# Rotary turn in a two-layer hybrid kernel: rows swapped by SBUF transfers in place of a product with a constant matrix

## The chip, the cores and the metric

The kernel runs on one core of a Trainium2 chip, as one launch. The metric is the time on the device in microseconds (us); less is better. The engines are named as in the profile: PE (TensorE, matrix products), PEld (its weight loads), DVE (VectorE), ACT (ScalarE), POOL (GpSimd) and SP (SyncE, which here only issues transfers).

## What is computed

Two layers run over 512 latent tokens and 256 context tokens of width 1024. Each layer is: a half-step SwiGLU, a token mixer, and a second half-step SwiGLU, each with a modulation in front and a layer norm behind. Mixer 0 is a neighbourhood attention. Mixer 1 is a windowed attention of 16 query heads over 4 key heads, and its queries and keys are turned by a rotary embedding that depends on the row and the column of the token:

```python
def rot(xa, pos):
    ang = pos[:, None] * inv_freq[None, :]
    cos = jnp.cos(ang)[None, :, None, :].astype(x.dtype)
    sin = jnp.sin(ang)[None, :, None, :].astype(x.dtype)
    x1, x2 = xa[..., :n], xa[..., n:]
    return jnp.concatenate([x1 * cos - x2 * sin, x2 * cos + x1 * sin], axis=-1)

return jnp.concatenate([rot(x[..., :half], rows), rot(x[..., half:], cols)], axis=-1)
```

A head has 64 dimensions; `half` is 32 and `n` is 16. So within every block of 32 dimensions the upper 16 and the lower 16 change places, those that move up take a minus sign, and the result is multiplied by the sine; the tile itself, multiplied by the cosine, is added. Everything is float32 in the reference.

## The kernel before

Activations lie with the feature dimension on the 128 partitions and the tokens along the free dimension. Large products are done in three passes (`mm3`, lines 162 to 166): both factors are split into a high and a low part of a faster type, and high x high, high x low and low x high are summed in PSUM. Weights come from HBM in quarters of 128 x 512 (256 KB) through SP's queue (`raw_quarter`, line 94), and are split by ACT (line 102) and POOL (line 104) into a ring of eight pairs; five raw buffers (`RAWS`) and this ring (`RING`) set how far SP can load ahead.

Mixer 1 is `wa_mixer`. Its stages:

- V of the latent tokens (`v_tiles`), then two K tiles of 128 x 512 (two heads each), each projected (`wk`, lines 163 to 166), turned by `rope`, split and copied to both halves of the partitions by `stack_k` (lines 845 to 849);
- `proj(0)`: two Q tiles (`wq`), each turned by `rope` and split by `stack_q` (lines 838 to 841); then K and V of the context tokens (`wkc`, `vw`). In this stage the layer norm of the context tokens and its modulation (lines 317 to 322, 480) also run;
- for `u` from 0 to 2: attention of two head pairs with the Q at hand (`attn`: score products at lines 1156 to 1163 and 853/854, softmax on DVE and ACT, scaling at line 893, transposes at line 877, products with V at line 886), then `proj(u + 1)`, two more Q tiles, then the output projection of the heads that were just done (`wo_pairs`, tile `pow`, lines 163 to 166, added to the residual at line 495);
- attention of the last two head pairs and their output projection.

So `rope` is called ten times: for two K tiles and eight Q tiles. It copies the projection from PSUM to SBUF with its scale (`qe`, ACT, line 1098), multiplies the constant matrix `rm_sb` (a signed permutation, 128 x 128, float32) with it on PE (line 1100, the result in the PSUM bank pair `mm`, which the projections use too), multiplies that by the sine table `rc[1]` on DVE (line 1102), multiplies `qe` in place by the cosine table `rc[0]` on POOL (line 1103), and adds the two on DVE (line 1104).

The order of the instructions on every engine and on SP's queue is not the order of the source. The framework plans it before the run with a timing model of its own (`schedule_with_timeline_sim=True`): an instruction is placed when the model has its inputs and its buffer ready, earlier lines of the source first. On the chip every engine, and SP, then goes through its list strictly in order, and waits where an input is late. The helper `behind` adds constraints on the order, and `plan`/`at` put pieces of the layer norms at named points.

Constants are loaded by `constants()`, called by `late_gate` in the first SwiGLU (`ffn("0a", ...)`), while `gemv_dve`, a background stream of DVE products for the modulation (line 211), runs. That stream keeps two PSUM banks, tags `o` and `t`, for the conditioning vector (`cb`, written by ACT at line 235); the tag `t` has a single bank.

Temporary tiles of 128 x 512 come from pools by tag: `t2` has six buffers, `ln` two (`t2()`, lines 53 and 54).

Of the kernel before, what the change touches and what calls it, by code (L numbers as in the profile page):

```python
# [8 lines left out]
F32 = mybir.dt.float32  # L9
# [4 lines left out]
ALU = mybir.AluOpType  # L14
# [4 lines left out]
P = 128  # L19
D = 1024  # L20
# [18 lines left out]
def hybrid_kernel(ctx: ExitStack, tc: tile.TileContext, h0, cc, crow, wmod, wmodt, bmod, lnp, wst,  # L39
                  rpbp, nmask, sinks, ropec, rmat, ident, wmask, out):  # L40
    nc = tc.nc
    cp = ctx.enter_context(tc.tile_pool(name="cp", bufs=1))
# [7 lines left out]
    def bank(tag, nm):  # L50
        return pp.tile([P, 512], F32, tag=tag, name=nm, bufs=banks[tag])

    def t2(nm, tag="t2"):
        return tp.tile([P, 512], F32, tag=tag, name=nm, bufs={"t2": 6, "ln": 2, "sl": 2}[tag])
# [11 lines left out]
    nmask_sb = cp.tile([P, 3, 32], F32, name="nmask_sb")  # L66
    nsink = cp.tile([P, NH], F32, name="nsink")
    rm_sb = cp.tile([P, P], F32, name="rm_sb")
    onesd = cp.tile([P, P], F32, name="onesd")
    nc.vector.memset(onesd[:], 1.0 / D)  # L70
    zero = cp.tile([P, 4], F32, name="zero")
# [266 lines left out]
    def behind(x, y):  # L338

        if y is not None and x.ins.engine == y.ins.engine:  # L340
            tc.add_manual_dep(x.ins, y.ins.name, mybir.DependencyInfo(
                mybir.DependencyClass.NoSync, mybir.DependencyReason.DATA), reason="order")
# [559 lines left out]
    def constants():  # L902
        for t, src in ((lnp_sb, lnp), (nmask_sb, nmask), (rm_sb, rmat)):
            behind(nc.sync.dma_start(t[:], src[:]), loaded[0])
        nc.sync.dma_start(nsink[:], sinks[:].broadcast_to([P, NH]))
        nc.vector.tensor_scalar(out=nsink[:], in0=nsink[:], scalar1=-1.0, scalar2=None, op0=ALU.mult)

    def bias_tables():
        for r in range(8):
            behind(nc.sync.dma_start(xd[:, r], rpbp[:, :, 7 - r:15 - r]), loaded[0])  # L910
# [173 lines left out]
    def wa_mixer(gt):  # L1084
        phase("S")
        rc = []
        for i in range(2):
            t = gp.tile([P, NL], F32, tag="gs", name=f"rc{i}", bufs=6)
# [3 lines left out]
        nc.sync.dma_start(mk[:, 0:256], wmask[:])  # L1092
        nc.vector.tensor_copy(mkb[:].rearrange("p a b -> p (a b)"), mk[:, 0:256])

        def rope(nm, ps, scale):

            qe = t2(f"qe{nm}")
            nc.scalar.activation(qe[:], ps[:], AF.Copy, scale=scale)
            pr = bank("mm", f"pr{nm}")
            nc.tensor.matmul(pr[:], rm_sb[:], qe[:], start=True, stop=True)  # L1100
            sn = t2(f"sn{nm}")
            nc.vector.tensor_tensor(out=sn[:], in0=pr[:], in1=rc[1][:], op=ALU.mult)
            nc.gpsimd.tensor_tensor(out=qe[:], in0=qe[:], in1=rc[0][:], op=ALU.mult)
            nc.vector.tensor_tensor(out=sn[:], in0=qe[:], in1=sn[:], op=ALU.add)
            return sn

        iv = wpos[0]
        vt = v_tiles("w", wunit(), range(4), ("mm", "c"))
# [2 lines left out]
        for i in range(2):  # L1111
            ps = bank("s", f"wk{i}")
            mmk(ps[:], w, i * P, 0, NL)
            at(f"wk{i}")
            stack_k(*ks[i], 0, NL, rope(f"k{i}", ps, 1.0))

        def proj(u):
            w = wunit()
            qs = []
            for i in range(2):  # L1120
                ps = bank("mm", f"wq{u}_{i}")
                mmk(ps[:], w, i * P, 0, NL)
                at(f"wq{u}_{i}")
                sl = [slab(f"wq{u}_{i}_{x}") for x in range(2)]
                stack_q(*sl, 0, NL, rope(f"q{u}_{i}", ps, -0.125), 1.0)
                qs.append(sl)
            return qs

        qs = proj(0)
        for i in range(2):  # L1130
            ps = bank("mm", f"wkc{i}")
# [121 lines left out]
    with tc.tile_pool(name="pre", bufs=1) as fp:  # L1253
        open_av()
        for q in range(4):
            pieces = []
            for i in range(2):
                t = fp.tile([P, 4, 512], F32, tag="wm", name=f"wm0_{q}_{i}", bufs=7)
# [75 lines left out]
    def late_gate():  # L1334
        gemv_dve(0, (16, 20, (0, 1)), (20, 24, (0, 1)), (40, 72, (0, 1)), (24, 40, (0, 1)))
        for _ in range(33):
            next(bg[0][1])
        bg[0] = (bg[0][0] - 33, bg[0][1])
        constants()

    def whole(x, head):
# [23 lines left out]
    plan(wo6_2=l4[0][:1], wo6_3=l4[0][1:2], wm7_3=l4[0][2:3], pow3_1_256_1=l4[0][3:4], pow3_1_256_5=l4[0][4:6],  # L1365
         pow3_1_256_7=l4[1][:1])
    wa_mixer(gate(1, 5, 1.0))
    plan(pa1b_0_0_0=l4[0][6:], pv1b_0_0_0=l4[1][1:3], pd1b_0_0_3=l4[1][3:4], pd1b_0_0_7=l4[1][4:])
    ffn("1b", g1, lambda: gate(1, 8, 0.5), None, final, apart=True)
# [126 lines left out]
```

## Time and profile before

| | |
|---|---|
| time, median of 3 runs | 2771.27 us (2769.65 to 2777.23) |
| span of the profiled execution (from the first to the last instruction; the page gives no other time of it) | 2767.9 us |
| PE busy, share of the span | 2668.7 us, 96% |
| DVE busy | 1869.2 us, 68% |
| POOL busy | 1683.2 us, 61% |
| ACT busy | 1202.4 us, 43% |
| mean granted TensorE clock | 0.987 |
| first and last start of a rotary product | 2089.9 us and 2294.9 us |

All times in the profile are microseconds from the start of the span, unless marked ns. In rows of instructions, the first number is the start and the second the duration, then engine, line, operation, `output<-inputs`, shapes, and `xcount` where several were merged; square brackets give the idle time of the engine just before and what ended it. A name followed by `q` (SPq, ACTq) is the engine's queue: the issue of a transfer, not the transfer. Matmuls are pipelined, so their durations overlap; the distance from one start to the next is the cost of one. The clock is granted by a throttle; 1.00 is full speed.

### The profile page before, as it was taken

To read this page: it belongs to the slowest core of one execution; us is meant where nothing else is said; L and a number is where in the kernel's file an instruction comes from. 1 tells how busy PE (TensorE), PEld (TensorE's weight loads), DVE (VectorE), ACT (ScalarE), POOL (GpSimd) and SP (SyncE) were. 2 spreads that over 40 slices of the span, in tenths; PEclk is the share of its full clock that TensorE was granted. 3 is DMA by queue.
4 is the path that set the end of the run, shared out by engine and by line. 5 is a ranking of instruction groups with operands and counts; after the bars stand their busy time and mean duration, and the time that the engine had idled before them with its cause. 6 is when DMAs were issued, how large, how long until landed. Compare 5 with 4: busy or idle time off the path is not lost. (4 is left out here: it accounts for less than half of the span.)

```text
span 2767.9 us, 47921 instructions
## 1 busy us (share of the span) xinstructions
PE 2668.7 (96%) x16954; PEld 2419.6 (87%) x16954; DVE 1869.2 (68%) x4252; ACT 1202.4 (43%) x2487; POOL 1683.2 (61%) x1530
## 2 busy tenths in 40 slices
PE   8999999999999989999999999999998999899997
PEld 5899998888888888999998899999986777889997
DVE  4877777775555677656556676666587667787765
ACT  4344343366446353443433434343336555444442
POOL 4786766454434556967665577767545445677762
PEclk9999999999999999999999999999999999999998
DMA  9467565421222113454543226465722111235551
GB/s 317 108 172 206 143 157 155 143 81 58 58 58 64 55 49 89 121 136 117 133 133 103 72 85 164 123 163 158 208 83 61 31 32 47 70 96 126 134 143 56
DMA packets 295615, 311.92 MB, mean 113 GB/s; under 512 B 27856, under 2 KB 193872, under 8 KB 294352
## 3 DMA queue, kind: packets, MB, share of 16 engines
q1 hardware_dynamic: 278960, 279.36, 33.5%
q0 software_dynamic: 16128, 29.37, 6.4%
q8 instruction: 134, 2.20, 0.3%
q14 instruction: 105, 0.86, 0.1%
q10 hardware_dynamic: 288, 0.14, 0.0%
HBM read 300.92 MB, written 12.25 MB: 113 GB/s over the span
## 5 line engine op out<-in xcount | busy, mean ns | idle before, releaser
L104 POOL TENSOR_TENSOR wl<-wr,wh 128x512 fp32r<-128x512 f32 x200 | 262.9, 1332 | 148.8 <-ACT wh L102 93.3
L104 POOL TENSOR_TENSOR wl_s<-S,wh_s 128x512 fp32r<-128x512 f32 x240 | 317.7, 1359 | 49.5 <-ACT wh_s L102 48.2
L102 ACT CAST wh_s<-S 128x512 fp32r<-128x512 f32 x256 | 155.3, 620 | 418.2 <-POOL S L620 137.4
L620 POOL TENSOR_TENSOR S<-wr,wr 128x512 f32<-128x512 f32 x128 | 174.2, 1361 | 184.5 <-DMA wr<-in_wst_dram 165.6
L211 DVE CUSTOM_DVE_ANT_0 jk<-wt,cb 128x512 f32<-128x512 f32 x360 | 244.5, 679 | 23.5 <-DMA wt<-in_wmodt_dram 18.6
L104 POOL TENSOR_TENSOR wl_a<-wr,wh_a 128x512 fp32r<-128x512 f32 x144 | 189.7, 1365 | 18.0 <-ACT wh_a L102 14.3
L102 ACT CAST wh_a<-wr 128x512 fp32r<-128x512 f32 x192 | 118.8, 621 | 147.1 <-PE pd1b L165 18.6
L102 ACT CAST wh<-wr 128x512 fp32r<-128x512 f32 x200 | 120.6, 617 | 82.7 <-DMA wr<-in_wst_dram 20.0
L495 DVE SCALAR_TENSOR_TENSOR z<-pd0b,gt,z 128x256 f32<-128x256 f32 (+1 forms) x168 | 97.2, 594 | 42.3 <-PE pd0b L166 41.7
L495 DVE SCALAR_TENSOR_TENSOR z<-pd1a,gt,z 128x512 f32<-128x512 f32 (+1 forms) x160 | 95.6, 614 | 38.5 <-PE pd1a L166 38.2
L893 POOL TENSOR_SCALAR p<-p,l 128x512 f32<-128x512 f32 x64 | 44.3, 694 | 120.3 <-DVE l L1001 114.6
L495 DVE SCALAR_TENSOR_TENSOR z<-pd0a,gt,z 128x512 f32<-128x512 f32 (+1 forms) x160 | 93.5, 611 | 16.2 <-PE pd0a L166 16.1
L335 POOL TENSOR_SCALAR z<-z,ag_None,ab_None 128x256 f32<-128x256 f32 (+1 forms) x78 | 62.3, 802 | 62.1 <-DVE uh L321 47.9
L620 POOL TENSOR_TENSOR S<-S,wr 128x512 f32<-128x512 f32 x64 | 90.5, 1414 | 3.2 <-POOL x1b L562 0.4
L620 POOL TENSOR_TENSOR S<-wr,S 128x512 f32<-128x512 f32 x64 | 90.1, 1408 | 3.5
L893 POOL TENSOR_SCALAR pw<-pw,l 128x512 f32<-128x512 f32 (+1 forms) x64 | 41.0, 641 | 67.2 <-DVE l L1195 24.1
L317 ACT ACTIVATE ufl<-z,bi_None,sc_None 128x256 f32<-128x256 f32 (+1 forms) x86 | 55.1, 655 | 53.6 <-DVE z L480 52.4
L1000 ACT ACTIVATE p<-s,m 128x512 f32<-128x512 f32 x64 | 44.0, 688 | 78.1 <-DVE m L998 72.2
L322 DVE TENSOR_TENSOR ul<-ufl,uh 128x256 fp32r<-128x256 f32 (+1 forms) x88 | 59.9, 687 | 2.6 <-ACT ufl L317 1.3
L211 DVE CUSTOM_DVE_ANT_0 jk<-zspare,cb 128x512 f32<-128x512 f32 x88 | 59.7, 678 | 0.6
L495 DVE SCALAR_TENSOR_TENSOR z<-pd1b,gt,z 128x512 f32<-128x512 f32 (+1 forms) x91 | 53.2, 618 | 9.1 <-PE pd1b L166 8.9
L104 DVE TENSOR_TENSOR wl_a<-wr,wh_a 128x512 fp32r<-128x512 f32 x48 | 53.8, 1134 | 6.7 <-ACT wh_a L102 6.7
(1469 smaller groups left out, 10671.7 us busy)
## 6 DMA issues: line engine op xcount, KB each, us to landing
wr<-in_wst_dram SPq DMA_DIRECT2D x456, 256.0 KB
wt<-in_wmodt_dram SPq DMA_DIRECT2D x206, 256.0 KB
zspare<-in_wmodt_dram SPq DMA_DIRECT2D x50, 256.0 KB
wr_0b<-in_wst_dram SPq DMA_DIRECT2D x47, 256.0 KB
wr_1b<-in_wst_dram SPq DMA_DIRECT2D x47, 256.0 KB
wr_2b<-in_wst_dram SPq DMA_DIRECT2D x47, 256.0 KB
wr_3b<-in_wst_dram SPq DMA_DIRECT2D x47, 256.0 KB
wm<-in_wmod_dram SPq DMA_DIRECT2D x8, 1024.0 KB
```

Of the source, the lines that this page charges most:

```text
L102: nc.scalar.copy(hi[:], src[:])
L104: x = eng.tensor_tensor(out=lo[:], in0=src[:], in1=hi[:].bitcast(F32), op=ALU.subtract)
L211: x = nc.vector.tensor_tensor_reduce(out=junk[:], in0=w[:], in1=cb[st], scale=1.0, scalar=0.0, op0=ALU.mult, op1=ALU.add, accum_out=out[st])
L317: nc.scalar.activation(uf[:, :n], zs, AF.Identity, scale=s1, bias=s2)
L322: return hi, nc.vector.tensor_tensor(out=lo, in0=uv, in1=uo.bitcast(F32), op=ALU.subtract)
L335: nc.gpsimd.tensor_scalar(out=zs, in0=zs, scalar1=prm[2][:, d:d + 1], scalar2=prm[3][:, d:d + 1], op0=ALU.mult, op1=ALU.add)
L495: last[0] = nc.vector.scalar_tensor_tensor(out=zt(d, c0, c1), in0=pd, scalar=gt[:, d, st:st + 1], in1=zt(d, c0, c1), op0=ALU.mult, op1=ALU ...
L620: nc.gpsimd.tensor_tensor(out=t[:], in0=a[:], in1=b[:], op=o)
L893: nc.gpsimd.tensor_scalar(out=p, in0=p, scalar1=r, scalar2=0.0, op0=ALU.mult, op1=ALU.add)
L1000: last_exp[0] = nc.scalar.activation(p[:], ps[:], AF.Exp, bias=m[:, 0:1], scale=-1.0, accum_out=l[:, 0:1])
```

## The change

The matrix product is gone from `rope`. In its place SP issues eight transfers for each tile, from SBUF to SBUF: block `x` of 16 partitions of the new tile `qr` is filled from block `x ^ 1` of `qe`, which is 16 partitions of 2 KB, 32 KB, a transfer. The sine product on DVE then reads `qr` from SBUF instead of the PSUM bank, and writes it in place; POOL writes the cosine product to a tile of its own, `qc`, from the pool `ln`.

The sign, which the matrix held, goes into the sine table: `rc[1]` is multiplied once by a column `sgn` of +1 and -1 on POOL. That column is made in `constants()` by a product of `rm_sb` with a column of `onesd` (whose elements are 1/D) in a bank with the tag `t`, multiplied by D on DVE. The inputs of the kernel and its host code stay as they are.

```diff
@@ constants of the kernel
     rm_sb = cp.tile([P, P], F32, name="rm_sb")
+    sgn = cp.tile([P, 1], F32, name="sgn")
     onesd = cp.tile([P, P], F32, name="onesd")
@@ constants()
         nc.vector.tensor_scalar(out=nsink[:], in0=nsink[:], scalar1=-1.0, scalar2=None, op0=ALU.mult)
+        ps = bank("t", "sgn")
+        nc.tensor.matmul(ps[:, 0:1], rm_sb[:], onesd[:, 0:1], start=True, stop=True)
+        nc.vector.tensor_scalar(out=sgn[:], in0=ps[:, 0:1], scalar1=float(D), scalar2=None, op0=ALU.mult)
@@ wa_mixer()
+        nc.gpsimd.tensor_scalar(out=rc[1][:], in0=rc[1][:], scalar1=sgn[:], scalar2=0.0, op0=ALU.mult, op1=ALU.add)
+
         def rope(nm, ps, scale):
 
-            qe = t2(f"qe{nm}")
+            qe, qr, qc = t2(f"qe{nm}"), t2(f"qr{nm}"), t2(f"qc{nm}", "ln")
             nc.scalar.activation(qe[:], ps[:], AF.Copy, scale=scale)
-            pr = bank("mm", f"pr{nm}")
-            nc.tensor.matmul(pr[:], rm_sb[:], qe[:], start=True, stop=True)
-            sn = t2(f"sn{nm}")
-            nc.vector.tensor_tensor(out=sn[:], in0=pr[:], in1=rc[1][:], op=ALU.mult)
-            nc.gpsimd.tensor_tensor(out=qe[:], in0=qe[:], in1=rc[0][:], op=ALU.mult)
-            nc.vector.tensor_tensor(out=sn[:], in0=qe[:], in1=sn[:], op=ALU.add)
-            return sn
+            for x in range(8):
+                nc.sync.dma_start(qr[16 * x:16 * x + 16, :], qe[16 * (x ^ 1):16 * (x ^ 1) + 16, :])
+            nc.gpsimd.tensor_tensor(out=qc[:], in0=qe[:], in1=rc[0][:], op=ALU.mult)
+            nc.vector.tensor_tensor(out=qr[:], in0=qr[:], in1=rc[1][:], op=ALU.mult)
+            nc.vector.tensor_tensor(out=qr[:], in0=qr[:], in1=qc[:], op=ALU.add)
+            return qr
```

## Prediction, on record before the result

> **What bounds the kernel now.** I read the head of the page and its chain of waits first, then the busy time of each engine in stretches around mixer 1, then the lines of the rotary turn one by one, and last the timeline around one turn, with SP's queue.
>
> ```profile
> span 2767.9 us, 47921 instructions
> PE 2668.7 (96%) x16954; PEld 2419.6 (87%) x16954; DVE 1869.2 (68%) x4252; ACT 1202.4 (43%) x2487; POOL 1683.2 (61%) x1530
> GB/s 317 108 172 206 143 157 155 143 81 58 58 58 64 55 49 89 121 136 117 133 133 103 72 85 164 123 163 158 208 83 61 31 32 47 70 96 126 134 143 56
> PE 34%; DVE 6%; ACT 1%; issue 1%; DMA 1%; POOL 1%; DVEq 0%; ACTq 0%; POOLq 0%; SPq 0%
> ```
>
> PE is busy for 96% of the span and holds most of the chain, so a PE instruction less is time less wherever PE has no wait of its own. That has to be asked stage by stage. Columns of the next view: stretch in us, its length, busy us (and instructions) of PE, PEld, DVE, ACT, POOL, then the granted clock, the DMA share and GB/s.
>
> ```profile
> 2094.18:2102.44 8.26, 4.38 (x22) 3.39 (x20) 5.47 (x13) 8.01 (x13) 0.00 (x0) 1.00 0.01 2
> 2097.97:2101.85 3.88, 0.00 (x0) 0.00 (x0) 2.57 (x6) 3.74 (x8) 0.00 (x0) 1.00 0.00 0
> 2101.85:2105.65 3.80, 3.80 (x9) 2.48 (x10) 2.75 (x7) 3.77 (x8) 2.48 (x3) 0.59 0.00 0
> 2177.29:2190.00 12.71, 12.38 (x66) 9.46 (x65) 11.73 (x24) 7.78 (x22) 8.07 (x8) 1.00 0.32 95
> 2190.00:2228.00 38.00, 37.16 (x309) 29.31 (x309) 23.40 (x72) 20.20 (x64) 14.95 (x24) 1.00 0.07 21
> ```
>
> There are two kinds of stage. In the first, where the two K tiles and the first two Q tiles are turned, ACT is busy for 8.01 of 8.26 us and PE stands for 3.88 us; afterwards the clock is granted at 0.59 for 3.80 us. ACT bounds this stage. In the stages around the other six Q tiles (2190 to 2228 stands for them) PE is busy for 37.16 of 38.00 us: PE bounds these.
>
> **The turn, before.**
>
> ```profile
> L1100 PE MATMUL prq<-qeq,rm_sb x16: 590/592/902, 2101.9 to 2294.9; 128*128 128x512 f32 x16
> L1100 PE MATMUL prk<-qek,rm_sb x4: 592/592/676, 2089.9 to 2091.2; 128*128 128x512 f32 x4
> L1102 DVE TENSOR_TENSOR snq<-prq,rc x8: 676/680/690, 2103.8 to 2296.8; 128x512 f32<-128x512 f32 x8
> L1104 DVE TENSOR_TENSOR snq<-qeq,snq x8: 678/691/843, 2106.0 to 2298.3; 128x512 f32<-128x512 f32 x8
> ```
>
> ```profile
> 2169.99 0.60 ACT L1098 ACTIVATE qeq<-wq 128x512 f32<-128x512 f32 x1 [7.32 <-PE wq L166]
> 2170.84 1.13 PE L1100 MATMUL prq<-qeq,rm_sb 128*128 128x512 f32 x2
> 2172.04 0.40 PE L165 MATMUL wq<-ul,wh 128*128 128x512 f32 x1
> 2172.27 0.40 PE L166 MATMUL wq<-uh,wl 128*128 128x512 f32 x1
> 2173.39 0.69 DVE L1104 TENSOR_TENSOR snq<-qeq,snq 128x512 f32<-128x512 f32 x1 [0.54 <-POOL qeq L1103]
> 2174.77 1.72 DVE L840 SCALAR_TENSOR_TENSOR wq<-snq,wq 64x512 fp32r<-64x512 f32 x2 [0.70 <-ACT wq L839]
> 2175.25 5.23 SPq L94 DMA_DIRECT2D wr<-in_wst_dram  x4
> 2177.29 0.28 PE L1156 MATMUL sw<-wk,wq 128*128 128x256 f32 x1
> 2178.96 1.02 PE L1100 MATMUL prq<-qeq,rm_sb 128*128 128x512 f32 x2
> 2180.05 0.39 PE L165 MATMUL pow<-wol,wh 128*128 128x512 f32 x1
> ```
>
> **Step 1, removed: ten products on PE.** Each is two matmul records. Matmuls of 512 columns follow each other by 0.23 us (2172.04 to 2172.27), and one of them stands between the product and the row quoted behind it. So the first product costs 2172.04 - 0.23 - 2170.84 = 0.97 us and the second 2180.05 - 0.23 - 2178.96 = 0.86 us. I take 0.9: 9.0 us in all, 5.4 for the six tiles of the PE-bound stages and 3.6 in the ACT-bound stage. Only the 5.4 I count as reaching the end. The PSUM bank of each product falls away too, so the next output projection can start a bank sooner; I count nothing for it.
>
> **Step 2, added: eight transfers a tile, on the way to the scores.** No transfer from SBUF to SBUF is in this trace. The nearest rows are an issue of a small load, and the first load of the kernel with the instruction that waited for it:
>
> ```profile
> 36.78 0.33 SPq L904 DMA_DIRECT2D nmask_sb<-in_nmask_dram  x1
> 37.15 0.43 SPq L904 DMA_DIRECT2D rm_sb<-in_rmat_dram  x1
> 0.75 0.39 SPq L58 DMA_DIRECT2D c_sb<-in_cc_dram  x1
> 3.20 0.42 ACT L75 ACTIVATE c_sb<-c_sb 128x256 f32<-128x256 f32 x1 [0.24 <-DMA c_sb<-in_cc_dram]
> ```
>
> An issue takes 0.33 to 0.43 us; I take 0.43 from one to the next. From issue to use is 3.20 - 0.75 = 2.45 us. The last of eight is therefore usable 7 x 0.43 + 2.45 = 5.5 us after the turned tile's copy (qe) ends, and two DVE operations of 0.68 and 0.69 us follow: 6.8 us. Before, it was 2173.39 + 0.69 - 2170.59 = 3.5 us. A tile comes 3.3 us later. (Bounds of the transfers: 0.33 spacing and a landing in half the time, 3.5 us; each one after the other, below.)
>
> Who waits? The first score product of the next head pair stands at 2177.29; its Q was finished at 2174.77 + 1.72 = 2176.49. Afterwards Q is finished at 2179.8, and PE, 0.9 us sooner, arrives at 2176.4: 3.4 us too early. What can cover it is the output projection of the heads before:
>
> ```profile
> L163 PE MATMUL pow<-woh,wh x16: 388/396/798, 2179.4 to 2195.3; 128*128 128x512 f32 x16
> ```
>
> 16 sums of three products each, 48 x 0.23 = 11.0 us, none of which needs the new Q. The order on PE is fixed before the run by a planner that estimates the transfers; if it estimates them short, score products come ahead of the projection and PE stands for up to 3.4 us. I take 0.7 us for each of three stages (one bank of the projection, 6 x 0.23 = 1.4 us, and more stand ahead in most orders), +2.1, with 0 and +10.2 as bounds. The second tile of each pair is first read by the head pair after that, some 19 us later (half of the stretch from 2190 to 2228), and costs nothing; without that cover it would cost the same 3.3 us.
>
> **Step 3, the ACT-bound stage.**
>
> ```profile
> 2088.65 1.07 ACT L1098 ACTIVATE qek<-wk 128x512 f32<-128x512 f32 x2
> 2092.38 1.76 DVE L1104 TENSOR_TENSOR snk<-qek,snk 128x512 f32<-128x512 f32 x1 [0.19 <-POOL qek L1103]
> 2094.18 0.62 ACT L846 CAST wk<-snk 64x512 fp32r<-64x512 f32 x1 [4.46 <-DVE snk L1104]
> ```
>
> ACT's run begins at 2094.18 with the first turned K tile. Its copy ends at about 2089.2; with 5.5 us of transfers and 1.4 us on DVE the run begins at 2096.1, 1.9 us later. ACT can fill 0.6 us of that with the copy of the first Q tile, which PE has ready sooner: +1.3. Bounds: the second K tile's eight issues stand behind the first's, another 3.4 us if ACT's order waits for them (+5.3); or all of PE's gain counts, with its stand and the slow clock behind it (0.41 x 3.80 = 1.6): -3.6 - 3.9 - 1.6 = -9.1.
>
> **Step 4, SP's queue.** All 80 transfers go on the queue that loads the weights.
>
> ```profile
> SPq L94 <- POOL wl L104: 76.2, 17, 40.8
> ```
>
> SP stands in front of a weight load for up to 40.8 us until POOL frees a buffer; in the stage above it stood until 2175.25. The first tile's eight issues, from 2170.6 to 2174.0, fit ahead of it: 0. The second tile's fall among the four loads from 2175.25 on and can put the last ones off by 3.4 us; the loads fill a ring used one projection later, so 0 again, with +1 a stage as the upper bound should ACT's weight casts come to wait.
>
> **Step 5, the sign.** One product of 128 by 1 and its scaling now lie in the first FFN, in a PSUM bank that a background stream holds until it changes halves:
>
> ```profile
> 266.46 0.60 ACT L235 ACTIVATE cb<-cr 128x512 f32<-128x512 f32 x1 [0.17 <-DVE ga L211]
> L893 POOL TENSOR_SCALAR p<-p,l 128x512 f32<-128x512 f32 x64 | 44.3, 694 | 120.3 <-DVE l L1001 114.6
> ```
>
> There ACT waited for DVE by 0.17 us only, so PE would hardly wait longer: +0.4, from 0 to +2. The sine table is multiplied once by POOL (0.69 us by the second row) in the time before the first K tile is ready; were POOL late there, it would cost its 0.69.
>
> **Step 6, DVE and POOL.** The sine product reads SBUF instead of PSUM: 0.69 for 0.68 us, +0.1 over ten. The add, which already reads two SBUF tiles, took 1.76 us once (2092.38) beside POOL's cosine product; were the sine product always caught so, DVE would lose up to 1.08 us a tile, part of it under PE's work. POOL writes a tile of its own and no longer waits for PE.
>
> [...]
>
> Sum: -5.4 + 2.1 + 1.3 + 0 + 0.4 + 0.1 = -1.5 us. The profiled span of 2767.9 us becomes 2766.4; the page gives no other time of that execution, the median shown, 2771.27, stands 3.4 us above its span, and I carry this over: **2770 us**.
>
> **Rivals.**
> *All of PE's gain counts.* For it: PE at 96%, and a stand of 3.88 us whose cause is one of these products. Against it: ACT's 8.01 of 8.26. Time: -9.0 - 3.9 - 1.6 = -14.5, 2757.
> *Slower: PE stands in front of the first score product.* The planner places it early and Q lands late, in three stages: 3.4 us and then a slow clock like the one measured (1.6), 5.0 each, and the first stage at its upper bound: -5.4 + 15.0 + 5.3 = +14.9, 2786. For it: only 0.8 us lay between Q and its use (2176.49, 2177.29). Against it: 11.0 us of projection. It decides as soon as PE's stand exceeds the 1.8 us that two products free in a stage.
> *Slower still: the transfers go one after the other.* 8 x 2.45 = 19.6 us a tile; Q would be ready 14.1 us later than in step 2, at 2193.9, against a projection that ends at 2187.4: 6.5 us for each of three stages, and 14.1 + 1.3 in the first, less 5.4: +29.5, 2801. Against it: 317 GB/s in the first slice is 256 KB in 0.8 us, so transfers do overlap. [...] Here each is 32 KB on its own 16 partitions; the trace of before can't say.
>
> **How the numbers follow.** A measurement of this kernel tells about 0.3% (8 us) from no change, 2763 to 2779.6. Forecast 0.48, with a range of its own from 2764 to 2777; the gain in full 0.22; PE's stand 0.25; one after the other 0.05. So faster 0.22, same 0.48, slower 0.30. From 2756 to 2789 the range holds all but the last rival and the tails.
>
> **What would show it.** Right: no rotary product on PE; some 5 us from the qe copy to DVE's sine product; in the stages of the last six tiles no stand of PE over 1 us ahead of the scores; ACT's run starting about 2 us later behind the K copies. Wrong: PE idle on Q's second-half write at the first score product, a clock under 1 behind it; SP's weight loads late so that ACT's casts wait for DMA; landing times far from 2.45 us; or another order of the whole program, since the planner plans all of it anew.

## The result

| | time, median of the runs | span of the profiled execution |
|---|---|---|
| before | 2767.21 us (2762.99 to 2777.23, 6 runs) | 2767.9 us |
| changed | 2780.94 us (2779.81 to 2786.72, 6 runs) | 2782.8 us |

The ratio is 1.0048, with a 95% interval from 1.0029 to 1.0066: the changed kernel is slower by 13.3 us (0.0048 x 2768). The forecast was 2770 us, no change.

The head of the changed kernel's page:

```profile
span 2782.8 us, 48095 instructions
PE 2669.1 (96%) x16936; PEld 2421.1 (87%) x16936; DVE 1883.9 (68%) x4253; ACT 1202.4 (43%) x2487; POOL 1689.9 (61%) x1531
```

PE is busy as long as before (2668.7 us then), although ten products are gone. Behind the first split of mixer 1 (a mark explained below) it is even busier, 202.60 us against 198.22, at a mean clock of 0.98 against 1.00: the half clock shown below took back at least a part of what the products had freed. DVE works 14.7 us more (1869.2 then), 8.7 of them in mixer 1.

Where in the program does the time go? The first product of mixer 1 (`vw`), the splits of its heads (`woh`) and the first product behind it (`pa1b`), first in the kernel before, then in the changed one. After the colon stand the shortest, median and longest duration in ns, then the first and the last start:

```profile
L163 PE MATMUL vw<-wh,uh x32: 277/283/420, 2059.2 to 2080.5; 128*128 128x256 f32 x32
L889 ACT CAST woh<-wo x10: 353/585/603, 2152.2 to 2351.2; 128x512 fp32r<-128x512 f32 x6, 128x256 fp32r<-128x256 f32 x4
L163 PE MATMUL pa1b<-uh,wh x64: 278/283/579, 2361.0 to 2425.4; 128*128 128x256 f32 x64
```

```profile
L164 PE MATMUL vw<-wh,uh x32: 277/283/385, 2055.1 to 2075.4; 128*128 128x256 f32 x32
L890 ACT CAST woh<-wo x10: 352/588/596, 2149.6 to 2364.3; 128x512 fp32r<-128x512 f32 x6, 128x256 fp32r<-128x256 f32 x4
L164 PE MATMUL pa1b<-uh,wh x64: 278/283/475, 2374.0 to 2438.1; 128*128 128x256 f32 x64
```

The changed kernel enters the mixer 4.1 us ahead and leaves it 13.0 us behind: the mixer takes 318.9 us instead of 301.8. Up to the first split, the stage that ACT bounds, it loses 1.5 us (94.5 against 93.0). The other 15.6 us are lost behind it, in the stages where the six later tiles of Q are turned and used.

Each run left one trace, and in all of them the first mark lies between 2048.6 and 2060.3 us, so the 4.1 us say nothing of the change. The time between the marks moves less: with the sign alone (below) the mixer takes 304.0 us, 94.8 and 209.2 in the two parts. Differences of some 2 us, the 1.5 us of the first part among them, can't be told from none.

Here is the first of these turns in the changed kernel's timeline; each row starts with its start and duration:

```profile
2167.97 0.60 ACT L1104 ACTIVATE qeq<-wq 128x512 f32<-128x512 f32 x1 [7.59 <-PE wq L167]
2168.59 4.93 SPq L1106 DMA_DIRECT2D qrq<-qeq  x8
2172.22 0.69 DVE L891 TENSOR_TENSOR wol<-wo,woh 128x512 fp32r<-128x512 f32 x1 [6.13 <-ACT woh L890]
2174.97 1.66 DVE L1108 TENSOR_TENSOR qrq<-qrq,rc 128x512 f32<-128x512 f32 x1 [2.06 <-DMA qrq<-qeq]
2176.65 0.40 PE L167 MATMUL pow<-woh,wl 128*128 128x512 f32 x1
2176.73 1.58 DVE L1109 TENSOR_TENSOR qrq<-qrq,qcq 128x512 f32<-128x512 f32 x1
2178.23 0.74 DVE L496 SCALAR_TENSOR_TENSOR zspare<-pow,gt,zspare 128x512 f32<-128x512 f32 x1
2179.03 0.50 PE L164 MATMUL pow<-woh,wh 128*128 128x512 f32 x1 [1.98 <-DVE zspare L496]
2183.47 0.28 PE L1161 MATMUL sw<-wk,wq 128*128 128x256 f32 x1
```

The copy ends at 2168.57. SP issues the eight transfers one behind the other in 4.93 us, and DVE starts the sine product 6.4 us after the copy. It stood 2.06 us for it, and in its order the accumulation of the output projection (`zspare<-pow`) comes behind the sine product and the add. The projection has two PSUM banks. PE fills both and then stands for 1.98 us until the first is read: its last product into that bank began at 2175.27, and DVE began to read it at 2178.23. When the scores begin at 2183.47, PE doesn't wait for Q at all. The granted clock around that stand:

```profile
2177.00:2179.60 2.60, 0.62 (x3) 0.48 (x3) 2.60 (x3) 1.23 (x2) 0.76 (x1) 0.99 0.53 178
2179.60:2183.00 3.40, 3.40 (x9) 2.63 (x8) 3.26 (x4) 0.64 (x2) 1.28 (x1) 0.50 0.45 105
2196.90:2200.00 3.10, 3.10 (x16) 2.46 (x13) 1.93 (x8) 1.92 (x9) 1.36 (x3) 0.50 0.00 0
```

PE runs at half clock for 3.40 us after the stand, and for another 3.10 us some 14 us later.

One whole stage, from the copy of its first Q tile to that of the next, cut into the first 7 us, the 21 us behind them and the rest; the kernel before, then the changed one:

```profile
2170.00:2177.00 7.00, 7.00 (x39) 5.44 (x38) 3.67 (x5) 4.20 (x7) 3.55 (x3) 1.00 0.07 20
2177.00:2198.00 21.00, 20.67 (x117) 16.50 (x116) 19.73 (x48) 12.52 (x36) 14.20 (x18) 1.00 0.28 82
2198.00:2227.70 29.70, 28.86 (x252) 22.18 (x253) 15.40 (x48) 15.23 (x47) 9.11 (x15) 1.00 0.03 10
```

```profile
2168.00:2175.00 7.00, 7.00 (x41) 5.53 (x40) 0.73 (x2) 3.94 (x7) 5.28 (x5) 1.00 0.19 42
2175.00:2196.00 21.00, 17.45 (x83) 13.18 (x82) 19.96 (x30) 8.70 (x21) 9.71 (x8) 0.92 0.39 110
2196.00:2231.90 35.90, 35.24 (x279) 27.51 (x280) 20.50 (x70) 19.25 (x63) 12.46 (x22) 0.95 0.01 2
```

The third number behind the length is DVE. In the middle 21 us it was full in the kernel before too: 19.73 us, while PE had 20.67. Both engines are full there, and only the mean over the stage looks like PE alone. The change leaves DVE with 0.73 us instead of 3.67 us of work in the first 7 us. A stretch that is full has no room to make this up. The work shows in the third part, 20.50 us instead of 15.40, and that part is 6.2 us longer.

### The profile page after: what moved, and what is told of

Its sections match the earlier page's. It is cut to its first block, busy times and chain, and to the rows that moved or that the text cites. A ratio compares the mean times of both kernels' runs of the same rounds, so it can differ in the third digit from the quotient of the medians.

```text
span 2782.8 us, 48095 instructions
## 1 busy us (share of the span) xinstructions
PE 2669.1 (96%) x16936; PEld 2421.1 (87%) x16936; DVE 1883.9 (68%) x4253; ACT 1202.4 (43%) x2487; POOL 1689.9 (61%) x1531
```

## The experiments

Theory T, after these traces: DVE, which works in order, stands for the transfers with the projection's accumulations behind it. R1: SP's queue. R2: DVE's operations with two operands in SBUF. R3: the sign and the new order that the planner makes. T2, C and R4 to R7 came later and are stated in the expectations. All ratios are against runs of the kernel before on the same chip; a ratio less 1, times 2768 us, gives the differences in us.

### The sign alone

```diff
+        ps = bank("t", "sgn")
+        nc.tensor.matmul(ps[:, 0:1], rm_sb[:], onesd[:, 0:1], start=True, stop=True)
+        nc.vector.tensor_scalar(out=sgn[:], in0=ps[:, 0:1], scalar1=float(D), ...)
...
+        for _ in range(2):
+            nc.gpsimd.tensor_scalar(out=rc[1][:], in0=rc[1][:], scalar1=sgn[:], ...)
```

> The kernel before with the sign part alone: the sgn column is made in the first FFN, and the sine table is multiplied by it twice, so that it ends as it was; TensorE's product with the constant matrix stays. Theory T (VectorE, which works in order, stands at the sine product for the transfers; the accumulations of the output projection stand behind it, TensorE's banks fill, and it stands and then runs at a lower granted clock): the sign has no part in this, so 2762 to 2769 us, the time before or up to 5 us less, as the changed kernel was 4.1 us ahead when its mixer 1 began. Rival R3 (the new instructions make the planner order the work otherwise, and this order costs the time): 2775 to 2781 us.

Measured: 2767.1 us, ratio 1.0006 [0.9991, 1.0020]. The sign costs nothing that can be told. R3 keeps only the order inside mixer 1.

### No transfers, and transfers that nobody reads

```diff
-            for x in range(8):
-                nc.sync.dma_start(qr[16 * x:16 * x + 16, :], qe[16 * (x ^ 1):16 * (x ^ 1) + 16, :])
-            nc.vector.tensor_tensor(out=qr[:], in0=qr[:], in1=rc[1][:], op=ALU.mult)
+            nc.vector.tensor_tensor(out=qr[:], in0=qe[:], in1=rc[1][:], op=ALU.mult)
```

> The changed kernel without the eight transfers: the sine product reads qe itself, so the swap of the rows is left out of the computation. T: VectorE finds its operand as soon as ScalarE has scaled it, about 6 us earlier a tile, the stands of TensorE at the output projection (5.1 us in 4 waits on zspare) are gone, and the two products that were removed in each stage come out as a gain: 2756 to 2765 us. Rival R2 (the sine product and the add, with two operands in SBUF, take longer beside GpSimd's product, 1.66 and 1.58 us, and that is the loss): these products stay, so 2774 to 2781 us. R3: 2775 to 2781 us. Rival R1 (the eight issues and transfers themselves delay SyncE's queue, the weight loads in it, or other transfers) gives the same as T here.

Second form: the loop stays, but its target is a DRAM tile, `jt`, in place of `qr`.

> As without the transfers, but the eight transfers are issued and go to a DRAM buffer that nobody reads; the sine product reads qe itself, so the swap of the rows is left out of the computation. SyncE and the DMA queues have their work, and VectorE has no wait for it. T: within 2 us of the kernel without transfers, 2756 to 2766 us. R1: 2775 to 2781 us, as in the changed kernel. R2 and R3: 2774 to 2781 us.

Measured: 2766.5 us, ratio 0.9999 [0.9982, 1.0016], without transfers; 2767.0 us, 1.0003 [0.9986, 1.0019], with transfers that nobody reads. The first two parts of a stage without transfers, its sum, and the issues of the second form:

```profile
2167.40:2174.40 7.00, 7.00 (x41) 5.52 (x40) 4.37 (x5) 4.43 (x8) 4.78 (x4) 1.00 0.18 51
2174.40:2195.40 21.00, 18.49 (x116) 15.04 (x116) 19.77 (x43) 11.89 (x35) 13.19 (x13) 1.00 0.27 77
sum 58.70, PE 55.24 PEld 43.36 DVE 40.98 ACT 31.51 POOL 28.37; mean PE 18.41 PEld 14.45 DVE 13.66 ACT 10.50 POOL 9.46
```

```profile
L1107 SPq DMA_DIRECT2D jtq<-qeq x64: 302/418/1290, 2101.1 to 2299.2; - x64
```

R1 falls: the issues (0.42 us each in this form) and the transfers on SP's queue cost nothing as long as nobody waits for them. The loss is in the wait. But both runs miss what T had for them by a little on the other side (2756 to 2765 and 2756 to 2766 us): PE has 1.3 us less work in the stage (55.24 against 56.53 us, the sum of the three parts before), and the stage is 1.0 us longer (58.7 against 57.7). DVE has 2.2 us more (40.98 against 38.80) and is full in the middle part, where PE gets only 18.49 of its 21 us.

### The sine product given to DVE later

```diff
+            def turned():
+                x = nc.vector.tensor_tensor(out=qr[:], in0=qr[:], in1=rc[1][:], op=ALU.mult)
+                if point:
+                    behind(x, last[0])
+                nc.vector.tensor_tensor(out=qr[:], in0=qr[:], in1=qc[:], op=ALU.add)
+                then(qr)
...
+                     f"pow{u - 1}_0_{(1, 5)[i]}" if u else None)
```

> The changed kernel, all of its computation, with VectorE's sine product, its add and the stacking of the new Q given to VectorE later: in stages 1 to 3 behind the second accumulation (first tile of Q) and the sixth (second tile) of the output projection, so that no accumulation stands behind the wait for the transfers. T: TensorE's stands on zspare (5.1 us in 4) vanish or fall under 1 us, VectorE's waits on the transfers (5.7 us in 3) fall under 2 us, 2760 to 2769 us. R1, R2 and R3: all that they blame stays, 2776 to 2783 us.

Measured: 2780.1 us, ratio 1.0050 [1.0031, 1.0070], as the changed kernel. One wait of PE, the middle part of the stage, and the stage's sum:

```profile
PE sw L1171 <- ACT pw L1196: 13.8, 10, 2.2
2170.90:2191.90 21.00, 16.76 (x80) 13.17 (x80) 17.83 (x34) 9.83 (x26) 10.44 (x10) 0.90 0.36 112
sum 64.10, PE 59.15 PEld 45.61 DVE 39.07 ACT 31.96 POOL 27.15; mean PE 19.72 PEld 15.20 DVE 13.02 ACT 10.65 POOL 9.05
```

PE's wait on `zspare` falls to 0.3 us in 1. The changed kernel has 5.1 us in 4 (first row). The second row is of the run with the late sine product again:

```profile
PE pow L164 <- DVE zspare L496: 5.1, 4, 2.0
ACT wq L840 <- DVE qrq L1113: 7.6, 3, 3.6
```

So the stand that T blames was removed, and the time didn't change. The stand moved to the score products, which now wait for ACT's exponentials (13.8 us in 10, against 2.7 in 5 in the changed kernel), and ACT stands for the turned tile, by up to 3.6 us at a time (3.1 in the changed kernel, 1.2 before). The slow clock came along (0.90 in the middle part). T falls as the whole cause. What part of the 13.3 us it carries isn't shown, because the edit also finishes the turned tile later: the add of the first tile ends 12.1 us behind the copy, in the changed kernel 9.7 us. Hence T2: what costs is that Q is late, wherever something waits for it.

### One transfer, four transfers, two queues

```diff
-            for x in range(8):
-                nc.sync.dma_start(qr[16 * x:16 * x + 16, :], qe[16 * (x ^ 1):16 * (x ^ 1) + 16, :])
+            nc.sync.dma_start(qr[:], qe[:])
```

> The changed kernel with one transfer of all 128 partitions in place of the eight; the rows are not swapped, so the rotation is left out of the computation. Theory T2, put in T's place after the late-sine run (2780.1 us, where the stand moved from the output projection to the score products): what costs is that the new Q is late, wherever the order lets something wait for it; TensorE runs out of other work, stands, and a stand of about 2 us brings a stretch at half clock. One issue instead of eight takes 7 x 0.63 = 4.4 us off the 6.4 us from the scaled tile to the sine product, which leaves about 2 to 3 us; TensorE's longest stand in a stage should fall under 1.7 us (the longest that left the clock at 1.00 in the run without transfers): 2766 to 2771 us, VectorE's wait on the transfer at most 2 us a tile. Rival R4 (it is not the lateness but the presence of a transfer between ScalarE and VectorE, with an order of work that the planner builds around it): 2776 to 2782 us.

The run with four has `range(4)` and 32 in place of 16.

> The changed kernel with four transfers of 32 partitions each, which swap blocks of 32 rows instead of 16, so the rotation is not the reference's. T2: 4 x 0.63 = 2.5 us of issues are gone, about 3.9 us from the scaled tile to the sine product; a time between that with one transfer and that with eight, 2768 to 2776 us. R4: 2776 to 2782 us, as with eight.

The run with two queues keeps the eight:

```diff
-                nc.sync.dma_start(qr[16 * x:16 * x + 16, :], ...)
+                (nc.sync, nc.scalar)[x % 2].dma_start(qr[16 * x:16 * x + 16, :], ...)
```

> The changed kernel, all of its computation, with the eight transfers of a tile issued by SyncE and ScalarE in turn, four each. T2: the last is issued 4 x 0.63 = 2.5 us sooner, about 3.9 us to the sine product, as with four transfers; against it stand four issues a tile on ScalarE, 2.5 us of its time, in the first stage that ScalarE bounds (four tiles) as well: 2770 to 2779 us. R4: 2776 to 2783 us.

| transfers that DVE waits for | ratio, 95% interval | in us | turned tile, us behind its copy | mixer 1 in the trace, us |
|---|---|---|---|---|
| kernel before | 1 | 0 | 3.5 | 301.8 |
| none | 0.9999 [0.9982, 1.0016] | -0.3 | 3.7 | 305.5 |
| one | 1.0012 [1.0001, 1.0024] | +3.3 | 4.9 | 307.3 |
| four | 1.0028 [1.0015, 1.0041] | +7.8 | 7.0 | 315.7 |
| eight, two queues | 1.0020 [1.0009, 1.0030] | +5.5 | 8.1 | 311.5 |
| eight (the change) | 1.0048 [1.0029, 1.0066] | +13.3 | 9.7 | 318.9 |

The fourth column is the end of the add less the end of ACT's copy, for the first Q tile of the stage shown; the last is the time between the marks `vw` and `pa1b`.

Parts of a stage and its sum, with one transfer (first part), then with four (first and middle part, and a wait of PE between the first split and `pa1b`), then the sum with two queues:

```profile
2163.10:2170.10 7.00, 7.00 (x41) 5.53 (x40) 3.83 (x5) 3.85 (x7) 4.24 (x3) 1.00 0.33 99
sum 59.00, PE 56.58 PEld 43.58 DVE 40.57 ACT 32.12 POOL 27.89; mean PE 18.86 PEld 14.53 DVE 13.52 ACT 10.71 POOL 9.30
```

```profile
2173.80:2180.80 7.00, 7.00 (x41) 5.54 (x40) 2.48 (x3) 3.62 (x6) 5.08 (x4) 1.00 0.40 111
2180.80:2201.80 21.00, 18.37 (x104) 13.59 (x104) 20.08 (x36) 11.10 (x29) 10.56 (x10) 1.00 0.27 77
sum 60.60, PE 57.31 PEld 43.56 DVE 41.47 ACT 32.06 POOL 27.29; mean PE 19.10 PEld 14.52 DVE 13.82 ACT 10.69 POOL 9.10
PE sw L1161 <- DVE wq L841: 4.0, 3, 1.3
```

```profile
sum 60.80, PE 58.15 PEld 44.81 DVE 40.28 ACT 31.79 POOL 29.15; mean PE 19.38 PEld 14.94 DVE 13.43 ACT 10.60 POOL 9.72
```

All three came within what T2 had for them, and R4 falls. The more issues stand ahead of the sine product, the less DVE gets done in the first 7 us (4.37, 3.83, 2.48, 0.73 us with none, one, four and eight), and the longer the stage is (58.7, 59.0, 60.6, 63.9 us). With four, the clock is 1.00 in the middle part too, and the stage is nevertheless 2.9 us longer than before. PE hardly waits for `zspare` there (0.3 us in 1); its score products wait for Q itself, 4.0 us in 3. This is the plainest sight of T2 in these traces.

### The turn on GpSimd

```diff
-            nc.vector.tensor_tensor(out=qr[:], in0=qr[:], in1=rc[1][:], op=ALU.mult)
-            nc.vector.tensor_tensor(out=qr[:], in0=qr[:], in1=qc[:], op=ALU.add)
+            nc.gpsimd.tensor_tensor(out=qr[:], in0=qr[:], in1=rc[1][:], op=ALU.mult)
+            nc.gpsimd.tensor_tensor(out=qr[:], in0=qr[:], in1=qc[:], op=ALU.add)
```

> The changed kernel, all of its computation, with the sine product and the add on GpSimd instead of VectorE. The wait for the transfers then stands in GpSimd's order, and no accumulation of the output projection is behind it on VectorE. T (in-order wait on VectorE is what costs): 2762 to 2772 us. T2 (lateness of Q): the new Q is later still, 1.3 us or more for each of the two operations on GpSimd against 0.7 at best on VectorE, and GpSimd's splits of the weights (1.3 us each) stand behind the wait: 2779 to 2795 us.

Measured: 2779.6 us, ratio 1.0040 [1.0028, 1.0052].

```profile
sum 62.90, PE 59.77 PEld 46.48 DVE 35.32 ACT 31.91 POOL 32.20; mean PE 19.92 PEld 15.49 DVE 11.77 ACT 10.64 POOL 10.73
```

DVE has 5.9 us less to do in the stage than in the changed kernel (35.32 against 41.18) and no wait for a transfer, and the stage is only 1.0 us shorter. The first turned tile is finished 11.6 us behind its copy, 1.9 us later than in the changed kernel. Less work on DVE is no help where Q comes still later; this speaks against T as the whole cause once more, and against DVE's load as the whole cause.

### The stand filled with products

```diff
+            def filler(u=u, w=w, os=os):
+                ps = bank("s", f"fill{u}")
+                for j in range(8):
+                    x = nc.tensor.matmul(ps[:], rw(w, 0, P, 2 * P)[0], os[0][0][:, 0:NL], start=j == 0, stop=j == 7)
+                    if j == 0:
+                        behind(x, last_pe[0])
+                in_front[0] = x
+            if u < 2:
+                plan({f"pow{u}_0_1": [filler]})
```

> The changed kernel with eight products of 512 columns, which nobody reads, put on TensorE where it stood for 1.98 us in the second and third stage (between the second and the third sum of the output projection); the order around them stays. Eight take 8 x 0.23 = 1.8 us, as long as the stand. Theory C (part of the price of lateness is the half clock that follows a stand; in the changed kernel it covered about 3.4 us behind this stand and as much behind the next one in each of the two stages, half of which is lost): the granted clock stays at 1.00 behind the filled place, 1.7 to 3.3 us less a stage, 2774 to 2778 us though more work is done. Rival C' (the low clock has other reasons, or other work fills the time): no gain, 2780 to 2786 us.

Measured: 2785.9 us, ratio 1.0060 [1.0040, 1.0080]: no gain, and with its interval not to be told from the changed kernel. The two stages in the changed kernel, then with the stand filled:

```profile
2168.00:2231.90 63.90, 59.69 (x402) 46.22 (x401) 41.18 (x100) 31.88 (x90) 27.45 (x34) 0.95 0.15 42
2231.90:2294.10 62.20, 58.01 (x401) 44.86 (x400) 40.55 (x100) 31.79 (x90) 27.48 (x34) 0.97 0.16 44
```

```profile
2173.10:2236.60 63.50, 58.80 (x409) 45.21 (x408) 41.55 (x100) 31.92 (x91) 27.35 (x34) 1.00 0.15 42
2236.60:2302.00 65.40, 60.44 (x410) 46.48 (x409) 39.86 (x100) 31.93 (x91) 26.93 (x34) 0.97 0.15 42
```

In the second stage of the mixer the experiment did what it was made for: the clock is 1.00 throughout. That stage is 0.4 us shorter, although 3.25 us of half clock (half of 3.40 + 3.10) are gone and 1.8 us of products came in. PE, faster now, waits more (4.7 us not busy instead of 4.2). In the third stage the clock falls later all the same, and the stage is 3.2 us longer (65.4 against 62.2). C misses: the whole gained nothing, and where the half clock went, the stage hardly shortened. By this stage the half clock looks like a sign of the late tile and not like a price of its own. That rests on one trace, of the longest of six executions (2793.5 us).

### The sine product from PSUM, without transfers

```diff
-            nc.vector.tensor_tensor(out=qr[:], in0=qe[:], in1=rc[1][:], op=ALU.mult)
+            nc.vector.scalar_tensor_tensor(out=qr[:], in0=ps[:], scalar=scale, in1=rc[1][:], op0=ALU.mult, op1=ALU.mult)
```

> As the run without transfers (2766.5 us, no gain although TensorE lost ten products), with VectorE's sine product reading the projection's own PSUM bank; the swap of the rows is left out of the computation. R2 (the gain of the products was eaten since two operations of VectorE with both operands in SBUF run beside GpSimd's and take up to 1.75 us instead of 0.69): one of the two reads PSUM again and is ready 0.6 us sooner; 2760 to 2765 us. Rival R5 (the gain is eaten because the order makes TensorE wait for the accumulations on VectorE whatever the sine product takes): 2765 to 2769 us.

Measured: 2763.4 us, ratio 0.9983 [0.9968, 0.9997]. The sine product, first without transfers from SBUF, then from PSUM, and the sum of a stage and the three marks with the latter:

```profile
L1106 DVE TENSOR_TENSOR qrq<-qeq,rc x8: 691/781/1652, 2097.9 to 2292.6; 128x512 f32<-128x512 f32 x8
```

```profile
L1106 DVE SCALAR_TENSOR_TENSOR qrq<-wq,rc x8: 691/692/692, 2096.0 to 2286.7; 128x512 f32<-128x512 f32 x8
sum 57.70, PE 55.08 PEld 43.32 DVE 40.41 ACT 31.55 POOL 27.36; mean PE 18.36 PEld 14.44 DVE 13.47 ACT 10.52 POOL 9.12
L164 PE MATMUL vw<-wh,uh x32: 277/283/421, 2056.0 to 2077.2; 128*128 128x256 f32 x32
L890 ACT CAST woh<-wo x10: 350/586/590, 2145.8 to 2346.0; 128x512 fp32r<-128x512 f32 x6, 128x256 fp32r<-128x256 f32 x4
L164 PE MATMUL pa1b<-uh,wh x64: 274/283/552, 2355.8 to 2421.0; 128*128 128x256 f32 x64
```

R2 is borne out in part: reading one operand from PSUM, the product takes 0.69 us every time, and the kernel gains 4.7 us, with an interval from 0.8 to 8.9. Beside the run without transfers the intervals overlap, but in the traces the mixer takes 299.8 us against 305.5. The product doesn't start sooner: its first one in the stage shown starts 0.03 us behind the end of ACT's copy, as without transfers. The two rows differ in length as well: 0.69 to 1.65 us with both operands in SBUF, 0.69 us in all eight from PSUM. In the changed kernel's trace, the twelve sine products and adds of the six later Q tiles, all with both operands in SBUF, show the same: the five of 0.95 to 1.66 us overlap POOL's operations on 128x512 in time, and of the other seven, 0.68 or 0.69 us each, six ran while POOL stood. Before, three of the six later sine products, read from PSUM, ran within POOL's cosine product and took 0.68 us all the same (at 2172.17, for one, with POOL busy from 2172.05 for 1.30 us).

The gain isn't where step 1 of the prediction had it. The stage takes 57.7 us, as before, and all that lies behind the first split 210.0 us against 208.8. It is the part up to the first split that is shorter, 89.8 us against 93.0. The run with the sine product ahead of PE's product (below) keeps all ten products and has 90.4 and 210.2 us in its trace. So the traces don't show that the removed products brought anything; what these two runs share is a sine product that reads the projection's PSUM bank.

### The sine product ahead of the swap

```diff
-            nc.scalar.activation(qe[:], ps[:], AF.Copy, scale=scale)
+            nc.vector.scalar_tensor_tensor(out=qs[:], in0=ps[:], scalar=scale, in1=rc[1][:], op0=ALU.mult, op1=ALU.mult)
+            nc.scalar.activation(qc[:], ps[:], AF.Copy, scale=scale)
             for x in range(8):
-                nc.sync.dma_start(qr[16 * x:16 * x + 16, :], qe[16 * (x ^ 1):16 * (x ^ 1) + 16, :])
+                nc.sync.dma_start(qr[16 * x:16 * x + 16, :], qs[16 * (x ^ 1):16 * (x ^ 1) + 16, :])
...
-            nc.vector.tensor_tensor(out=qr[:], in0=qr[:], in1=rc[1][:], op=ALU.mult)
             nc.vector.tensor_tensor(out=qr[:], in0=qr[:], in1=qc[:], op=ALU.add)
```

> All of the computation, with the sine product ahead of the swap: VectorE multiplies the projection's PSUM bank by a sine table with the sign of the other row, the eight transfers on SyncE swap the product, and only the add follows them. T2: the chain behind the transfers is shorter by one operation of VectorE (0.7 to 1.7 us), the transfers take as long as in the changed kernel; between one and four transfers on the scale of lateness, less the stand at the sine product: 2770 to 2778 us. R4 (a transfer between two engines costs as such): 2777 to 2783 us.

And with the transfers on two queues, as above:

> As with the sine product ahead of the swap, with the transfers of a tile issued by SyncE and ScalarE in turn. T2: the issues take 2.5 us less (as the two queues did, which took the time from 2780.9 to 2772.2 us against 2768.5 of before), and one operation less follows: 2764 to 2771 us, about the time of the kernel before. To be faster than before it would have to be as early as without transfers; I don't expect that. R4: 2772 us or more.

Measured: 2771.4 us, ratio 1.0007 [0.9993, 1.0022], on one queue, and 2772.7 us, 1.0012 [0.9998, 1.0027], on two. A stage on one queue:

```profile
2171.70:2178.70 7.00, 7.00 (x41) 5.43 (x39) 1.75 (x3) 3.88 (x7) 5.66 (x5) 1.00 0.26 57
2178.70:2199.70 21.00, 20.45 (x124) 15.46 (x123) 20.41 (x44) 12.77 (x38) 12.63 (x14) 1.00 0.39 107
sum 58.40, PE 57.44 PEld 43.70 DVE 38.64 ACT 31.76 POOL 27.61; mean PE 19.15 PEld 14.57 DVE 12.88 ACT 10.59 POOL 9.20
```

With the same eight transfers on the same queue, one DVE operation moved from behind them to ahead of them brings back 1.0048 - 1.0007, 11 us; T2 had this, and R4 falls again. The move does two things at once, though: the operation leaves the chain behind the transfers, and it reads PSUM, where it takes 0.69 us every time. DVE does 2.5 us less in the stage (38.64 against 41.18), PE gets 20.45 of the middle 21 us instead of 17.45, the clock is 1.00. The trace is less kind than the ratio: between the marks the mixer takes 309.9 us, 8.1 more than before. The second queue, which took 8 us off the changed kernel, takes nothing off this one; T2 had expected 2764 to 2771 us, and missed. From the end of the sine product to the end of the add the first tile takes 7.9 us with two queues and 8.3 with one, not 2.5 us less: ACT issues its fourth transfer only 3.5 us after its first.

### Sine product ahead of PE's product, and transfers in the first stage only

The kernel before, with the sine product read from the projection's bank and the add from the product's bank:

```diff
-            nc.tensor.matmul(pr[:], rm_sb[:], qe[:], start=True, stop=True)
-            nc.vector.tensor_tensor(out=sn[:], in0=pr[:], in1=rc[1][:], op=ALU.mult)
+            nc.vector.scalar_tensor_tensor(out=sn[:], in0=ps[:], scalar=scale, in1=rc[1][:], op0=ALU.mult, op1=ALU.mult)
+            nc.tensor.matmul(pr[:], rm_sb[:], sn[:], start=True, stop=True)
...
-            nc.vector.tensor_tensor(out=sn[:], in0=qe[:], in1=sn[:], op=ALU.add)
+            nc.vector.tensor_tensor(out=sn[:], in0=qe[:], in1=pr[:], op=ALU.add)
```

> The kernel before, all of its computation, with no transfers: only the sine product moves ahead of TensorE's product, reads the projection's PSUM bank, and VectorE's add reads the product's PSUM bank. From the runs: the sine product from PSUM in place of two operands in SBUF was worth 3 us (2766.5 to 2763.4 us), and a turned tile that is ready one VectorE operation sooner was worth up to 9 us beside transfers. If lateness and two-operand operations are what the change lost by, this kernel, which has less of both than before, takes 2758 to 2766 us. Rival R6 (before, a tile is early enough, and the first stage is ScalarE's): 2766 to 2770 us, no change.

The changed kernel, with PE's product put back for the six later tiles of Q (`rope_dma` and `rope_pe` are the changed and the old `rope`):

```diff
         qs = proj(0)
+        nc.gpsimd.tensor_scalar(out=rc[1][:], in0=rc[1][:], scalar1=sgn[:], ...)
+        ropes[0] = rope_pe
```

> The changed kernel with the transfers only in the first stage (two tiles of K, the first two of Q); the six later tiles of Q are turned by TensorE's product and an unsigned sine table, all of the computation is done. By the marks in the traces the first stage lost 1.5 us and the later three 15.5 us. If the loss is in the stages of the six later tiles: 2766 to 2772 us. Rival R7 (the four tiles of the first stage, where ScalarE bounds the work, carry more of it, or set the order of the later stages): 2774 to 2781 us.

Measured: 2770.1 us, ratio 0.9998 [0.9986, 1.0010], and 2768.8 us, 0.9994 [0.9981, 1.0007]. A stage of the second:

```profile
2166.00:2223.60 57.60, 56.45 (x405) 43.95 (x402) 38.84 (x100) 32.04 (x91) 26.93 (x34) 1.00 0.14 37
```

With transfers in the first stage only the loss is gone, and the later stage shown takes 57.6 us, against 57.7 before: the six later tiles carry it, and R7 falls. The first run misses its 2758 to 2766 us: no change, as R6 had it. No kernel here that computes everything is faster than the kernel before; the one that is leaves the swap out.

## Why the prediction was wrong

**Step 1, ten products, -5.4 us.** The products are gone, but without any transfers the time didn't fall (0.9999), and behind the first split, where the 5.4 us were to come, no run without them is shorter than the 208.8 us of before (212.8 without transfers, 210.0 with the sine product from PSUM). What the latter gains in its trace, 3.2 us, lies in the first stage, and the run that keeps the products is shorter there too (90.4 us). The step took PE as the bound of the later stages from 37.16 of 38.00 us, while its own row of 2177.29 to 2190.00 has DVE at 11.73 of 12.71 us. PE is full there, and so is DVE, for about 21 us; that row was read for PE alone.

**Step 2, eight transfers, +2.1 us. This is the step that failed.** Its sizes were near: 6.4 us to the sine product instead of 5.5 (an issue every 0.62 us, (4.93 - 0.59) / 7, instead of 0.43; and 2.0 us from the last issue to use instead of 2.45). Its cover wasn't there. The 11.0 us of output projection don't read Q, as it said, but each sum needs a PSUM bank that DVE must have emptied, and DVE stood at the sine product; after two banks PE stood too. With the sine product put elsewhere in DVE's order, and the tile later for it, the time was the same. In place of 0.7 us, the stage shown lost 6.2 us (63.9 against 57.7), and all that lies behind the first split 15.6 us, beyond the step's upper bound of 10.2. PE's waits for the banks are 5.1 us of this; the rest isn't traced to single waits. That the second tiles wait for nothing was right: DVE's three waits for transfers (5.7 us) are those of the first tiles.

**Step 3, first stage, +1.3 us.** The marks in the two traces say +1.5, which can't be told from none; the run with transfers in this stage alone, 0.9994, shows no cost for the whole, and its trace +3.0 (96.0 against 93.0). Nothing speaks against the step, and nothing bears out its size.

**Step 4, SP's queue, 0.** Right: transfers that nobody reads cost nothing (1.0003).

**Step 5, sign, +0.4 us.** Nothing that can be told (1.0006 [0.9991, 1.0020]).

**Step 6, DVE and collisions, +0.1 us.** Mis-sized: the sine product took 1.66 us and the add 1.58 us in the turn shown, 0.9 to 1.0 us over what each took alone. Over the six later tiles of Q the two operations took 12.15 us against 8.66 before, 3.5 us more, which is within the step's bound of 1.08 us a tile; mostly it was the add that was caught (1.58 us or more in three of six), and the sine product in full only once. The step put this partly under PE's work. It had the collision, but not that DVE has little room for it.

**Rivals.** *PE's stand* named the kind of loss and nearly its size, 5.0 us a stage, 3.4 of stand and 1.6 of half clock, and 2786 us; in the changed kernel the stand was at the projection's banks, and in the run with the late sine product at the score products. That this rival stood at 0.25 rests on the cover. *All of PE's gain*: a third of its size appears once, only without the swap, and by the traces not through the products. *One after the other* didn't happen: the issues are serial, but what follows the last one is 2.0 us.

**What stays open.** The planner orders each of these kernels anew, and only in the run with the filled stand was the order meant to stay. How much of the 13.3 us is the late tile itself, how much DVE's longer work and how much an order that suits it badly isn't separated. With the sine product ahead of the swap the first turned tile is finished 8.3 us behind it, later than with four transfers (7.0 us behind the copy), and yet the stage is shorter (58.4 us against 60.6). So lateness orders the runs of the table that have one queue, but it isn't all.

## What to carry to other kernels

Before work is called cover for a late operand, follow it to the engine that empties its banks: if that engine is the one that waits, the cover is gone. Ask of each stage which engines are full in every part of it, since a stage at 98% of PE can hold 21 us in which DVE is full as well. What must pass through a chain of small transfers should leave as much as possible done ahead of them, and be measured once with the transfers taken out, because that is about the most the idea can bring.

## What the runs showed of the hardware

An issue on SP of 32 KB from SBUF to SBUF takes 0.59 us at the median, that of a small load 0.33 to 0.43 us, and that of the same 32 KB to DRAM 0.42 us:

```profile
L1106 SPq DMA_DIRECT2D qrq<-qeq x64: 512/587/1285, 2094.8 to 2306.0; - x64
```

One transfer of 256 KB was in use 2.27 us after its issue began, the last of eight of 32 KB after 2.04 us (2174.97 less 2172.93, the last issue's start): here the number of issues counts, not the bytes.

```profile
2163.76 0.47 SPq L1105 DMA_DIRECT2D qrq<-qeq  x1
2166.03 0.87 DVE L1107 TENSOR_TENSOR qrq<-qrq,rc 128x512 f32<-128x512 f32 x1 [4.51 <-DMA qrq<-qeq]
```

After a stand of 1.98 us, with PE busy for 0.62 of 2.60 us, the clock was at half for 3.40 us; after one of 1.32 us (up to 2196.14), for 3.10 us. In the run without transfers no part shown of a stage is under 1.00, with PE busy for 18.49 of 21 us and its longest wait for DVE in a stage 1.7 us:

```profile
PE pow L164 <- DVE z L496: 5.0, 3, 1.7
```

So the length of a single stand doesn't tell in these traces whether the clock falls.
